# A two-block transformer layer kernel: the last stage's fixed experts in plain float32, and its weight ring eleven tiles deep

## The chip, the cores and the metric

The kernel runs on one core of a Trainium2 chip. The metric is the device time of one execution in microseconds, given as the median of several executions. The profile shows another, single execution; its span runs from the first to the last instruction of the program.

## The reference

Two blocks follow each other on 256 tokens of 1024 features, all in float32. The first has two layers with a recurrent and gated-linear-attention mixer each, a dense feed-forward in the one layer and 8 experts of which 2 are chosen in the other. The second block has a differential-attention and retention mixer, and then the part that matters here, 64 experts of width 256, of which each token uses 8:

```python
scores = sigmoid(h @ router_w)
sel = scores + router_bias
top_e = top 8 of sel within the 4 best of 8 groups
wts = scores[top_e] / sum * 2.5
for each expert e, over its tokens xb:
    yb = (silu(xb @ w1[e]) * (xb @ w3[e])) @ w2[e]
    acc[tok] += yb * wt
out = rmsnorm(x + g2 * (acc + shared(h)))
```

Every expert's weights are 3 MB (w1 and w3 in two tiles of 1 MB, w2 in one), so this stage loads 192 tiles of 1024 KB, 201 MB of the 647 MB that the whole kernel moves.

## The kernel before

**Weights** come through a ring (class `Ring`, lines 246 to 331): `add` lists the tiles in the order of their use, `load` (L260 to L270) takes a buffer and issues one 1 MB transfer on SyncE's queue (L269). The ring has seven buffers (tag `ring`). SyncE runs on its own: it issues the next transfer when the buffer that it needs has been read for the last time, and when its queue has come to it.

**Split or plain.** A tile marked `split` is cut into two halves ("granules"). For each, ScalarE writes the upper part (L366) and VectorE the rest (L367) into a buffer with tag `wsp`, of which there are four (8 KB a partition each, as large as a ring buffer). A product is then three matmuls on float32r parts (`mm3`, L373 to L378). A tile not marked so is used as it is, in plain float32 matmuls.

**Blocks of experts.** The routing gives each expert a place by its load (`by_load`), the first `NSTAT` experts excepted, which keep fixed places in front. `blocks2` (L2115) makes blocks of 128 rows: each of the 3 fixed experts has a block of its own (capacity 128), then 9 experts with 96 rows, 25 with 64 and 27 with 32 are packed two, three or four to a block. That makes 29 blocks. Which expert stands at a place is known only after the routing: VectorE writes it to `order`, and SyncE reads it from there before it issues the first tile of that expert (`moe2_tiles`, L2144). Tiles of fixed experts need no `order`: 8 tiles of the stage come ahead of the first that does.

**The order in a block.** `experts` (L1158) runs the blocks. TensorE computes the first product (`eh`) in two halves, a tile of each expert per half, and then the second product (`ey`) of the block before. Between the quarter steps it puts other jobs (`slots`): the gather of the tokens of later blocks (`gps`, L1138, and the transpose `PTp`, L1106), the transpose of the activation (`gT`, L1187) and the scatter of finished blocks (`sc`, L1249). Blocks with one expert are "heavy" (split weights, products `eh<-wsp` and `ey<-wsp`); the others are "light" (plain, `eh<-ringw` L1281 and `ey<-ringw` L1207) and run two or four column strips of the array side by side.

**Around the routing.** `moe2` (L1983) computes the router, then the shared expert (3 split tiles), between whose parts the gather of the first two blocks stands. It then loads tiles ahead (`ahead(RING)`, L2086), reads the overflow flag (L2087) and branches (L2088): only if an expert has more tokens than its place holds, a loop over all 64 experts runs (`dense_fallback`, L1337). Behind the branch come the 29 blocks. The four `wsp` buffers join the ring there (`wide`), for tiles that are asked for when no split tile is left in the list.

Of the kernel before, what the change touches and what calls it, by code (L numbers as in the profile page):

```python
# [21 lines left out]
NU = 11  # L22
NSTAT = 3
NBIG2 = 9
NMID2 = 25
LEAD1 = 4
RING = 7
NSPLIT = 4
# [217 lines left out]
class Ring:  # L246
# [3 lines left out]
    def __init__(self, k):  # L250
        self.k, self.order, self.at = k, [], 0
        self.ready, self.raw, self.gran, self.half, self.hold = [], [], [], None, False
        self.busy = 0
        self.wide = False
        self.n = 0

# [3 lines left out]
    def load(self):  # L260
        src, split = self.order[self.at]
        self.at += 1
        if callable(src):
            src = src()
        wide = self.wide and self.half is None and not any(sp for _, sp in self.ready + self.order[self.at - 1:])
        tag, bufs = ("ring", RING) if not wide or self.n % (RING + NSPLIT) < RING else ("wsp", NSPLIT)
        self.n += wide
        w = self.k.sb.tile([128, 2048], F32, name="ringw", tag=tag, bufs=bufs)
        self.k.nc.sync.dma_start(w, src)  # L269
        self.ready.append((w, split))  # L270

    def ahead(self, n):
# [61 lines left out]
class K:  # L334
# [739 lines left out]
    def gather_jobs(self, mp, ps, blks, moe, npt=3):  # L1074


        V, S, T = self.V, self.S, self.T
        xnh, xnl, A, B = [moe[k] for k in ("xnh", "xnl", "A", "B")]
        nb, deep = len(blks), 2
        n = 128 * nb  # L1080
        light = [len(blk["cols"]) > 1 for blk in blks]
        R = {}
# [75 lines left out]
    def experts(self, steps, moe, mp, ps, queue, extra, tail, slots, ys=None):  # L1158
# [9 lines left out]
        pend = None  # L1168
# [9 lines left out]
        def second(st):  # L1178

            G, u, y, n = st["G"], st["u"], st["y"], st["n"]  # L1180
            np_ = len(st["b"]["cols"])
            tiles = self.col_tiles(st["b"])

            def flip():
                b = ps.tile([128, 2, 128], F32, name="gT", tag="t", bufs=2)
                for f in range(2):
                    T.transpose(b[:, f], G[:, 128 * f:128 * f + 128], self.ident)  # L1187
                if np_ > 1:
                    st["g"] = mp.tile([128, 2, 128], F32, name="ghf", tag="gh", bufs=2)
                    S.copy(st["g"], b)  # L1190
                else:
                    gh = mp.tile([128, 2, 128], F32R, name="gh", tag="gh", bufs=2)
                    gl = mp.tile([128, 2, 128], F32R, name="glo", tag="glo", bufs=2)
                    S.copy(gh, b)
                    V.tensor_tensor(out=gl, in0=b, in1=gh.bitcast(F32), op=OP.subtract)
                    st["g"] = (gh, gl)

            def go(mid=None):
                if np_ > 1:
                    w2 = [self.ring.get() for _ in range(np_)]  # L1200
# [53 lines left out]
        for s, blk in enumerate(steps):  # L1254
# [10 lines left out]
            x, cols = blk["x"], blk["cols"]  # L1265
            n = len(cols)
            light = n > 1
            hb = ps.tile([128, 512], F32, name="eh", tag="h", bufs=2)
            go = None
            if pend is not None:  # L1270
                flip, go = second(pend)
                urgent.insert(0, flip)
                heavy0 = len(pend["b"]["cols"]) == 1
            for half in range(2):
# [35 lines left out]
            pend = this  # L1310
# [335 lines left out]
    def blocks1(self):  # L1646

        return [dict(cols=((k, 128),)) for k in range(4)], [dict(cols=((k, 64), (k + 1, 64))) for k in (4, 6)]

# [333 lines left out]
    def moe2(self, st, ss):  # L1983
        nc, tc, V, S, T, I, sb = self.nc, self.tc, self.V, self.S, self.T, self.I, self.sb
        A, B = st["A2"], st["B2"]
        with self.pool("me") as mp, self.pool("mep", PSUM) as ps, self.pool("eg") as gp:
# [8 lines left out]
            with self.pool("sh") as sp, self.pool("rt") as rp:  # L1995
# [69 lines left out]
                b = ps.tile([128, 512], F32, name="gtp", tag="t", bufs=2)  # L2065
# [19 lines left out]
                self.ring.hold = False  # L2085
                self.ring.ahead(RING)  # L2086
            fl = nc.values_load(flag[0:1, 0:1], min_val=0, max_val=64)  # L2087
# [4 lines left out]
            with self.pool("ex") as ep:  # L2092
# [8 lines left out]
                queue = [(i, lambda i=i: self.gather_jobs(gp, ps, steps[i + 2:i + 4], moe)) for i in range(0, len(steps) - 2, 2)]  # L2101
                self.ring.wide = True
                self.experts(steps, moe, ep, ps, queue, None, tail, SLOTS2)
# [11 lines left out]
    def blocks2(self):  # L2115

        big, mid = [list(range(a, a + n)) for a, n in ((NSTAT, NBIG2), (NSTAT + NBIG2, NMID2))]
        low = list(range(NSTAT + NBIG2 + NMID2, N2))
        kinds = [[], [], [], []]
        for k in big:  # L2120
            kinds[0].append(((k, 96), (low.pop(), 32)))
        if len(mid) % 2:
            kinds[1].append(((mid.pop(0), 64), (low.pop(), 32), (low.pop(), 32)))
        while mid:
            kinds[2].append(((mid.pop(0), 64), (mid.pop(0), 64)))
        assert len(low) % 4 == 0
        while low:
            kinds[3].append(tuple((low.pop(0), 32) for _ in range(4)))
        seq = sorted(((i + (0.5, 0.5, 0.5, 0.1)[n]) / len(kind), c) for n, kind in enumerate(kinds) for i, c in enumerate(kind))
        return [dict(cols=c) for c in [((k, 128),) for k in range(NSTAT)] + [c for _, c in seq]]  # L2130

# [12 lines left out]
    def moe2_tiles(self, fixed):  # L2144
# [20 lines left out]
        for k, i in (seq[:cut] if fixed else seq[cut:]):  # L2165
            self.ring.add([tile_of(k, i)], split=k < NSTAT)

# [120 lines left out]
```

## Time and profile before

| what | value |
|---|---|
| median of 3 executions | 2045.52 us (2044.01 to 2047.15) |
| profiled execution, its own time | 2043.03 us |
| its span | 2041.3 us, mean granted clock 0.976 |
| busy share of the span | TensorE 93%, VectorE 55%, ScalarE 42% |
| stage of the 64 experts, first issue of a tile to the end | 1464.9 to 2041.3 us |

The times in the rows below count from the span's start. A matmul's duration in the rows includes its overlap with the next one, so the distance between the starts of two neighbours is what one costs. A float32 matmul appears as two records. An issue on SyncE is not the transfer: the transfer lands later. "idle before" names what the engine waited for last.

### The profile page before, as it was taken

The numbers are of one execution on the slowest core, as the hardware profiler recorded it, in microseconds if no ns is written. First come the engines' busy times: TensorE is split into PE (matmuls) and PEld (weight loads), VectorE is DVE, ScalarE is ACT, GpSimd is POOL, SyncE is SP. The second block draws the span as 40 slices with busy tenths as digits, with TensorE's granted clock in tenths as the row PEclk, the third lists the DMA queues.
The fourth block names the chain that finished last, engine by engine and source line by source line (L and its number), as shares of the span: only waits on it lengthen the run. The fifth ranks groups of instructions, "written<-read, shape, count | busy, mean of one in ns | idle before, by whom it ended". The sixth has DMA issues, their size and how long they took to land. (4 is left out here: it accounts for less than half of the span.)

```text
span 2041.3 us, 26923 instructions
## 1 busy us (share of the span) xinstructions
PE 1891.7 (93%) x10218; PEld 1169.4 (57%) x10218; DVE 1115.6 (55%) x1787; ACT 860.0 (42%) x1383; POOL 107.0 (5%) x80
## 2 busy tenths in 40 slices
PE   6999999999799999999999997999877999999998
PEld 3777878675565555656556544887655433433333
DVE  4566544565565565556565524545676554545444
ACT  3646554464474454554454523533444222211112
POOL 0002330101100000000000001000100000000000
PEclk8999999999699999999999998999988999999999
DMA  9765665666479999989999997433524999999996
GB/s 395 271 227 214 241 264 205 245 245 228 183 294 402 419 365 404 418 357 405 420 418 420 420 419 305 165 124 125 191 94 186 407 419 419 420 419 419 419 420 263
DMA packets 90348, 646.76 MB, mean 317 GB/s; under 512 B 10100, under 2 KB 10388, under 8 KB 12392
## 3 DMA queue, kind: packets, MB, share of 16 engines
q1 hardware_dynamic: 88128, 638.62, 78.2%
q0 software_dynamic: 1312, 4.46, 0.6%
q8 instruction: 82, 1.34, 0.3%
q10 hardware_dynamic: 776, 1.93, 0.2%
q14 instruction: 50, 0.41, 0.1%
HBM read 643.92 MB, written 1.05 MB: 316 GB/s over the span
## 5 line engine op out<-in xcount | busy, mean ns | idle before, releaser
L367 DVE TENSOR_TENSOR wsp<-ringw,wsp 128x1024 fp32r<-128x1024 f32 x431 | 518.9, 1228 | 321.7 <-ACT wsp L366 318.7
L366 ACT CAST wsp<-ringw 128x1024 fp32r<-128x1024 f32 x442 | 452.4, 1046 | 216.1 <-DMA ringw<-in_wm_dram 110.6
L1281 PE MATMUL eh<-ringw,xe 128*64 128x512 f32 (+1 forms) x1984 | 385.1, 602 | 17.1 <-DMA ringw<-in_we_dram 17.1
L1281 PEld LDWEIGHTS eh<-ringw,xe 128*64 128x64 f32 (+1 forms) x1984 | 96.6, 124 | 219.8 <-issue 182.4
L1207 PE MATMUL ey<-ringw,ghf 128*64 128x512 f32 (+1 forms) x992 | 184.7, 600 | 7.1 <-DMA ringw<-in_we_dram 5.6
L376 PE MATMUL eh<-wsp,xe 128*128 128x512 f32 x360 | 150.0, 417 | 1.8 <-DVEq L1599 1.4
L1150 ACT ACTIVATE xe<-gps,mod,A 128x256 f32<-128x256 f32 (+1 forms) x60 | 32.5, 542 | 269.9 <-DVE xe L1148 269.9
L377 PE MATMUL eh<-wsp,xe 128*128 128x512 f32 x360 | 143.1, 398 | 3.2 <-DVE wsp L367 3.2
L1250 DVE TENSOR_TENSOR x<-x,sc 128x512 f32<-128x512 f32 x132 | 85.5, 684 | 105.8 <-PE sc L1249 105.8
L378 PE MATMUL eh<-wsp,xe 128*128 128x512 f32 x360 | 143.0, 397 | 0.0
L1207 PEld LDWEIGHTS ey<-ringw,ghf 128*64 128x64 f32 (+1 forms) x992 | 50.3, 125 | 108.9 <-issue 92.0
L689 PE MATMUL ps_h<-wsp,acth 128*128 128x256 f32 x544 | 103.8, 291 | 1.3 <-DVE kdec L1861 0.8
L1138 PE MATMUL gps<-P,xnh 128*128 128x256 f32 (+1 forms) x336 | 87.7, 297 | 9.6 <-DVE P L1097 5.2
L689 PEld LDWEIGHTS ps_h<-wsp,acth 128*128 128x128 f32 x544 | 85.7, 194 | 14.2 <-issue 11.6
L1138 PEld LDWEIGHTS gps<-P,xnh 128*128 128x128 f32 x336 | 66.1, 197 | 39.5 <-issue 33.6
L376 PEld LDWEIGHTS eh<-wsp,xe 128*128 128x128 f32 x360 | 68.8, 191 | 31.0 <-ACT wsp L366 9.4
L1148 DVE TENSOR_SCALAR xe<-gps,A,mod 128x256 f32<-128x256 f32 (+1 forms) x68 | 34.3, 504 | 91.7 <-PE gps L1138 87.7
L1138 PE MATMUL gps<-P,xnl 128*128 128x256 f32 (+1 forms) x336 | 83.9, 285 | 0.0
L477 PE MATMUL ada<-ringw,cT 128*32 128x512 f32 x512 | 67.3, 629 | 14.4 <-DMA ringw<-in_wada_dram 7.4
L1230 ACT CAST yh<-yg 128x512 fp32r<-128x512 f32 x70 | 42.9, 619 | 85.3 <-DVE yg L1229 85.2
L377 PEld LDWEIGHTS eh<-wsp,xe 128*128 128x128 f32 x360 | 69.0, 192 | 17.1 <-DVE wsp L367 5.0
L689 PE MATMUL ps_h<-wsp,actl 128*128 128x256 f32 x272 | 77.7, 286 | 0.2 <-DVE actl L637 0.2
(472 smaller groups left out, 3159.8 us busy)
## 6 DMA issues: line engine op xcount, KB each, us to landing
ringw<-in_wm_dram SPq DMA_DIRECT2D x264, 1024.0 KB, 10.4
ringw<-in_we_dram SPq DMA_DIRECT2D x192, 1024.0 KB, 18.9
ringw<-in_wd_dram SPq DMA_DIRECT2D x80, 1024.0 KB, 6.0
ringw<-in_wada_dram SPq DMA_DIRECT2D x72, 1024.0 KB, 5.5
x<-in_x_dram ACTq DMA_DIRECT2D x1, 1024.0 KB
wab<-in_wab_dram POOLq DMA_DIRECT2D x2, 512.0 KB, 9.1
xc<-in_xc_dram POOLq DMA_DIRECT2D x1, 1024.0 KB, 5.4
fg<-in_fg_dram POOLq DMA_DIRECT2D x2, 512.0 KB, 4.0
```

The costliest lines, as they stand in the source:

```text
L366: self.S.copy(hi, w)
L367: (eng or self.V).tensor_tensor(out=lo, in0=w, in1=hi.bitcast(F32), op=OP.subtract)
L376: mm(out, x[0], w[0], start=start, stop=False, skip_group_check=True)
L377: mm(out, x[0], w[1], start=False, stop=False, skip_group_check=True)
L378: mm(out, x[1], w[0], start=False, stop=stop, skip_group_check=True)
L477: T.matmul(st["acc"][32 * j:32 * j + 32, :], self.cT[l // 2][:, 4 // n * i + j // n, :], w[:, 512 * j:512 * j + 512], start=i == 0, stop=l ...
L689: mm(ps[:, t, :], x[a], b[:, o:o + 256], start=(d == 0 and t == 0 and i == 0), stop=(d == 7 and i == 2), skip_group_check=True)
L1138: T.matmul(b[:, d - d0], xx[:, t, 128 * d:128 * d + 128], R["P"][:, t, :n], start=i == 0, stop=i == 3, skip_group_check=True)
L1207: mm(y[cc][o:o + w, :], g[:, f, o:o + w], w2[e][:, 1024 * f + 512 * cc:1024 * f + 512 * cc + 512], start=u == 0 and f == 0, stop=u == n - ...
L1230: S.copy(yh[:, c], yg[cc])
L1250: V.tensor_tensor(out=self.x[:, t, c], in0=self.x[:, t, c], in1=b, op=OP.add)
L1281: mm(hb[o:o + w, :], x[:, d, o:o + w], ws[e][:, 512 * k:512 * k + 512], start=d == 0, stop=d == 7, skip_group_check=True)
```

## The change

Three things are changed, all in the last stage:

1. `NSTAT` is 2 instead of 3 and `NMID2` 24 instead of 25. The third fixed expert takes a place by its load like the others. There are 28 blocks: 2 with one expert, and as before 26 with two to four, 5 of them with four (before: 4 with four and 1 with three).
2. Every block of the stage has `whole=True`: the two one-expert blocks use plain float32 tiles over the whole array, without any split. The one-expert blocks of the first block's experts (`blocks1`) keep their split.
3. The ring is widened to 11 tiles (7 `ring`, 4 `wsp` buffers) by a call ahead of the branch, and 11 tiles are loaded there instead of 7. Only 5 tiles come ahead of the first that needs `order`.

```diff
-NSTAT = 3
+NSTAT = 2
 NBIG2 = 9
-NMID2 = 25
+NMID2 = 24
...
-        wide = self.wide and self.half is None and not any(sp for _, sp in self.ready + self.order[self.at - 1:])
-        tag, bufs = ("ring", RING) if not wide or self.n % (RING + NSPLIT) < RING else ("wsp", NSPLIT)
-        self.n += wide
+        tag, bufs = "ring", RING
+        if self.wide is not None:
+            if self.wide >= RING:
+                tag, bufs = "wsp", NSPLIT
+            self.wide = (self.wide + 1) % (RING + NSPLIT)
...
+    def widen(self):
+
+        assert self.half is None and not any(split for _, split in self.ready + self.order[self.at:])
+        self.wide = len(self.ready) + len(self.raw)
...
-        light = [len(blk["cols"]) > 1 for blk in blks]
+        light = [blk["whole"] for blk in blks]
...
-                if np_ > 1:
+                if whole:
...
-            light = n > 1
+            light = blk["whole"]
...
                 self.ring.hold = False
-                self.ring.ahead(RING)
+                self.ring.widen()
+                self.ring.ahead(RING + NSPLIT)
             fl = nc.values_load(flag[0:1, 0:1], min_val=0, max_val=64)
...
-                self.ring.wide = True
...
-        return [dict(cols=c) for c in [((k, 128),) for k in range(NSTAT)] + [c for _, c in seq]]
+        return [dict(cols=c, whole=True) for c in [((k, 128),) for k in range(NSTAT)] + [c for _, c in seq]]
...
-            self.ring.add([tile_of(k, i)], split=k < NSTAT)
+            self.ring.add([tile_of(k, i)], split=False)
```

SyncE's queue just ahead of the branch, in the kernel before (`ringw` is a tile of the ring, `in_we_dram` the experts' weights; a DMA waits for the engines that last used its buffer): the last four fixed tiles, then the flag.

```order
L269 DMA ringw<-in_we_dram 128x2048 [waits DMAHW7_49,DVE_49,Pool_49]
L269 DMA ringw<-in_we_dram 128x2048 [waits DMAHW0_49,Pool_49]
L269 DMA ringw<-in_we_dram 128x2048 [waits DMAHW1_49,DVE_49]
L269 DMA ringw<-in_we_dram 128x2048 [waits DMAHW2_49,DVE_49]
L2087 TENSOR_LOAD flag [waits DVE_49]
L2087 ISA x2
L2088 COMPARE_AND_BRANCH
```

The same queue in the changed kernel: five fixed tiles and two tiles that need `order` are ahead of these rows, and the four here go into the `wsp` buffers.

```order
L270 DMA ringw<-in_we_dram 128x2048 [waits PE_49]
L2157 TENSOR_LOAD order
L2157 ISA x2
L270 ISA
L270 DMA ringw<-in_we_dram 128x2048 [waits DMAHW2_49,PE_49]
L270 ISA
L270 DMA ringw<-in_we_dram 128x2048 [waits DMAHW3_49,PE_49]
L270 ISA
L270 DMA ringw<-in_we_dram 128x2048 [waits DMAHW4_49,PE_49]
L2096 TENSOR_LOAD flag [waits DVE_49]
L2096 ISA x2
L2097 COMPARE_AND_BRANCH
```

So the tiles that were asked for behind the branch, one by one as split buffers came free, are asked for ahead of it, and wait for TensorE's last reads of the shared expert instead of for VectorE's splits.

TensorE in the kernel before, in the second block: the last of its 24 split products of `eh`, then the first of the 12 of `ey` for the block before it.

```order
L376 MATMUL eh<-wsp,acth 128x512
L377 MATMUL eh<-wsp,acth 128x512
L378 MATMUL eh<-wsp,actl 128x512
L376 MATMUL ey<-wsp,gh 128x512
L377 MATMUL ey<-wsp,gh 128x512
L378 MATMUL ey<-wsp,glo 128x512
```

TensorE in the changed kernel: the end of the first block, the whole second block, and the first quarter of the third, which has four experts (32-row strips).

```order
L1113 MATMUL PTp<-cst,Pg 128x128 x4
L1288 MATMUL eh<-ringw,xe 128x512 x4
L1194 MATMUL gT<-cst,G 128x128 x2
L1288 MATMUL eh<-ringw,xe 128x512 x6
L1214 MATMUL ey<-ringw,ghf 128x512 x4
L1288 MATMUL eh<-ringw,xe 32x512 x8
```

A one-expert block has 8 products of `eh` and 4 of `ey`, where it had 24 and 12.

## Rows read from the trace of the kernel before

**Rows 1.** The page, part 2: GB/s moved in each of the 40 slices.

```profile
GB/s 395 271 227 214 241 264 205 245 245 228 183 294 402 419 365 404 418 357 405 420 418 420 420 419 305 165 124 125 191 94 186 407 419 419 420 419 419 419 420 263
```

**Rows 2.** Busy time by stretch of the last stage: engines, clock, DMA share, GB/s.

```profile
core 0: us, PE busy (x) PEld busy (x) DVE busy (x) ACT busy (x) POOL busy (x), PEclk, DMA share, GB/s
1464.00:1499.00 35.00, 29.54 (x158) 19.01 (x150) 23.27 (x70) 17.40 (x29) 7.82 (x4) 0.95 0.45 180
1499.00:1520.00 21.00, 12.42 (x68) 10.04 (x67) 17.84 (x36) 12.59 (x25) 0.58 (x1) 0.83 0.27 82
1520.00:1568.00 48.00, 37.26 (x164) 28.48 (x168) 36.68 (x83) 24.37 (x43) 0.00 (x0) 0.90 0.46 173
1568.00:1593.00 25.00, 22.34 (x125) 9.34 (x118) 13.60 (x27) 7.47 (x15) 0.00 (x0) 0.93 0.72 286
1593.00:2017.00 424.00, 403.76 (x2460) 160.45 (x2458) 208.99 (x483) 82.38 (x190) 0.00 (x0) 1.00 1.01 419
2017.00:2041.00 24.00, 14.99 (x79) 5.72 (x76) 10.75 (x17) 7.46 (x16) 3.24 (x3) 0.88 0.23 93
```

**Rows 3.** SyncE's issues of tiles to 1520 us; ns, first and last start.

```profile
L269 SPq DMA_DIRECT2D ringw<-in_we_dram x8: 327/328/328, 1464.9 to 1518.3; - x8
...
DMA to landing us min/median/max: 4.8/5.8/9.7
```

**Rows 4.** SyncE's issues of tiles from 1593 us; columns as before.

```profile
L269 SPq DMA_DIRECT2D ringw<-in_we_dram x164: 332/333/1148, 1592.8 to 2005.2; - x164
```

**Rows 5.** Waits from 1513 to 1568 us: total us, times, longest us.

```profile
DVE wsp L367 <- ACT wsp L366: 6.6, 6, 2.2
...
PE eh L376 <- ACTq L2088: 6.3, 1, 6.3
```

**Rows 6.** VectorE's groups, 1513 to 1568 us: busy us, mean ns, idle before.

```profile
L367 DVE TENSOR_TENSOR wsp<-ringw,wsp 128x1024 fp32r<-128x1024 f32 x16 | 19.5, 1222 | 7.4 <-ACT wsp L366 6.6 <-DMA ringw<-in_we_dram 0.6
```

**Rows 7.** VectorE's timeline around the branch: start us, us, instruction.

```profile
1513.89 1.22 DVE L367 TENSOR_TENSOR wsp<-ringw,wsp 128x1024 fp32r<-128x1024 f32 x1
...
1517.02 1.22 DVE L367 TENSOR_TENSOR wsp<-ringw,wsp 128x1024 fp32r<-128x1024 f32 x1
...
1518.16 0.68 DVE L1109 TENSOR_SCALAR PT<-PTp 128x512 fp32r<-128x512 f32 x1
```

**Rows 8.** VectorE's timeline where the experts' order is written.

```profile
1498.26 0.21 DVE L1472 CAST order<-ordp 1x64 int32<-1x64 f32 x1
```

**Rows 9.** TensorE's timeline around the branch, with idle time in brackets.

```profile
1513.12 0.60 PE L1106 MATMUL PTp<-cst,Pg 128*128 128x128 f32 x4
1519.99 0.80 PE L376 MATMUL eh<-wsp,acth 128*128 128x512 f32 x1 [6.27 <-ACTq L2088]
```

**Rows 10.** TensorE's timeline in split blocks: single products.

```profile
1544.71 0.63 PE L376 MATMUL eh<-wsp,acth 128*128 128x512 f32 x1
1545.13 0.63 PE L377 MATMUL eh<-wsp,acth 128*128 128x512 f32 x1
...
1548.54 0.39 PE L376 MATMUL eh<-wsp,acth 128*128 128x512 f32 x1
1548.76 0.39 PE L377 MATMUL eh<-wsp,acth 128*128 128x512 f32 x1
```

**Rows 11.** TensorE's timeline: four plain float32 products over the whole array.

```profile
1493.58 3.59 PE L529 MATMUL ada<-adrow,cst 128*128 128x512 f32 x8
```

**Rows 12.** The chain of waits, 1495 to 1600 us: start us, us, what.

```profile
1563.23 1.88 PE gps L1138 x16
```

**Rows 13.** TensorE's timeline in blocks of plain float32 experts.

```profile
1567.85 1.92 PE L1281 MATMUL eh<-ringw,xe 128*32 128x512 f32 x16
...
1624.13 1.89 PE L1281 MATMUL eh<-ringw,xe 128*64 128x512 f32 x8
...
1639.68 1.90 PE L1281 MATMUL eh<-ringw,xe 128*32 128x512 f32 x16
```

**Rows 14.** TensorE's timeline at the stage's end.

```profile
2022.11 5.51 PE L1207 MATMUL ey<-ringw,ghf 128*32 128x512 f32 x32
```

More of the change, by code (lines that the diff above doesn't have):

```diff
@@ L253, in __init__ @@
         self.busy = 0
-        self.wide = False
-        self.n = 0
+        self.wide = None
     def add(self, srcs, split=True):
@@ L1180, in second @@
             G, u, y, n = st["G"], st["u"], st["y"], st["n"]
-            np_ = len(st["b"]["cols"])
+            np_, whole = len(st["b"]["cols"]), st["b"]["whole"]
             tiles = self.col_tiles(st["b"])
@@ L1198, in go @@
             def go(mid=None):
-                if np_ > 1:
+                if whole:
                     w2 = [self.ring.get() for _ in range(np_)]
@@ L1272, in experts @@
                 urgent.insert(0, flip)
-                heavy0 = len(pend["b"]["cols"]) == 1
+                heavy0 = not pend["b"]["whole"]
             for half in range(2):
@@ L1646, in blocks1 @@
     def blocks1(self):
-        return [dict(cols=((k, 128),)) for k in range(4)], [dict(cols=((k, 64), (k + 1, 64))) for k in (4, 6)]
+        return ([dict(cols=((k, 128),), whole=False) for k in range(4)],
+                [dict(cols=((k, 64), (k + 1, 64)), whole=True) for k in (4, 6)])
     def steps1(self):
@@ L2118, in blocks2 @@
         low = list(range(NSTAT + NBIG2 + NMID2, N2))
[L2119 to L2123, printed above, removed]
+        kinds = [[((k, 96), (low.pop(), 32)) for k in big], [], []]
         while mid:
-            kinds[2].append(((mid.pop(0), 64), (mid.pop(0), 64)))
-        assert len(low) % 4 == 0
+            kinds[1].append(((mid.pop(0), 64), (mid.pop(0), 64)))
         while low:
-            kinds[3].append(tuple((low.pop(0), 32) for _ in range(4)))
-        seq = sorted(((i + (0.5, 0.5, 0.5, 0.1)[n]) / len(kind), c) for n, kind in enumerate(kinds) for i, c in enumerate(kind))
-        return [dict(cols=c) for c in [((k, 128),) for k in range(NSTAT)] + [c for _, c in seq]]
+            kinds[2].append(tuple((low.pop(0), 32) for _ in range(4)))
+        seq = sorted(((i + (0.5, 0.5, 0.1)[n]) / len(kind), c) for n, kind in enumerate(kinds) for i, c in enumerate(kind))
+        return [dict(cols=c, whole=True) for c in [((k, 128),) for k in range(NSTAT)] + [c for _, c in seq]]
     def units(self, src, n, between=None):
```

## The prediction

> **What bounds the kernel now.** I read the slices first. In the last nine or so, from the stage of the 64 experts on, the rate stands at 419 to 420 GB/s, and the slice before them falls to 186 [rows 1]. So the question is when the stream of the stage becomes full and what keeps it from that. The stretches of the stage answer the first half: from 1593 to 2017 us the DMA share is 1.01 at 419 GB/s, while it is 0.27, 0.46 and 0.72 in the three stretches from 1499 to 1593 [rows 2]. A tile of 1024 KB is 1.049 MB, so at 419 GB/s one lands every 2.50 us. SyncE's issues confirm that tiles are then asked for as fast as they can come: 164 of the 192 are issued from 1592.8 to 2005.2 us, one per 2.5 us [rows 4].
>
> How far is the stream at 1593? Behind that, 424 us at 419 GB/s are 177.7 MB or 169.4 tiles; the last stretch moves 2.2 MB, of which 1.05 MB is the output, so another 1.1 tiles [rows 2]. Of 192, then, 170.5 are still to come and 21.5 have landed. Whatever makes this count larger at 1593 takes 2.50 us per tile off the end, as long as the stream stays full and TensorE keeps up behind it.
>
> What holds the stream back before 1593 is the second half. Only 8 tiles are issued to 1520 us, with up to 4.8 us (alone) to 9.7 us to land [rows 3]: that is all that seven buffers and the splits allow. Then the three split blocks run at the pace of VectorE and ScalarE: 16 splits of 1.22 us on VectorE between 1513 and 1568, which wait 6.6 us for ScalarE's half [rows 5, 6], and a ring buffer comes free only when its tile has been split. Three such blocks take from 1519.99 to 1567.85 us, 48 us [rows 9, 13]. TensorE itself is idle for 6.3 us at the branch [rows 5, 9].
>
> **The change, part by part.**
>
> *Removed splits.* No tile of the stage is split any more; what is left of these instructions belongs to the shared expert. The two splits of 1.22 us that stand ahead of the branch on VectorE (1513.89, 1517.02) delay `PT` at 1518.16 [rows 7], ScalarE's sums follow it, and TensorE's first product waits for them until 1519.99 [rows 9]. Without both, TensorE starts 2.4 us earlier, at 1517.5. It can't start ahead of 1513.7, where its own work ends, and it need not be later than now: bounds 1513.7 and 1520.
>
> *Plain products.* A split product costs 0.23 us (1548.54 to 1548.76), and twice that at the lower clock (1544.71 to 1545.13, 0.42) [rows 10]. A one-expert block has 36: 8.2 us. Four plain float32 products over the whole array take 3.59 us as a group with the tail of the last, 0.85 us each [rows 11]; a block has 12: 10.2 us. The Trainium skill, page "FP8 and Floating Point Precision", section "TensorE Precision Notes", says that true float32 makes four passes through the array. This speaks against the change, and the two rows agree with it (0.85 against 0.23): if TensorE's products set the time, two blocks would cost 4 us more than two split ones. But they don't set it here: three split blocks are 25 us of products in a stretch of 48 us, and it is the rest that goes.
>
> *First block.* 8 products of `eh` at 0.85 are 6.8 us; the gather of the next two blocks is 32 `gps` at 0.118 (16 in 1.88 us [rows 12]), 3.8 us; the transposes 0.5 us. TensorE comes from a pause, and the granted clock was 0.90 in the stretch from 1520 [rows 2], so I add 2 us for products at 1.2 GHz. Sum 13 us: 1517.5 to 1530.5. *Second block:* 6.8 us, the transpose 0.4 us and 4 products of `ey`, 3.4 us: to 1541.1. *Third block* (four experts): its first half is two quarters of 1.9 us [rows 13] and a transpose of 0.4 us, to 1545.4.
>
> *The ring.* VectorE writes `order` at 1498.5 [rows 8], as before. From there SyncE asks for tiles 6 to 11; the last two need the buffers that TensorE reads last for the shared expert, ahead of the row at 1513.12 [rows 9], so they go at about 1514 and land by 1520. Nothing is issued on the queue in front of them that is late. The first of the three moved tiles loses something: tile 6 was issued at 1484.2 and now waits for `order` until 1499, but is needed only at 1541; cost nothing. From then on tile k+11 is asked for when tile k has been read: 12 to 16 one by one through the first two blocks, and 17 to 20 together at 1545.4, when the first half of the third block is done. This is where the stream becomes full: 17 lands at 1545.4 + 4.8 = 1550.2, and 20 at 1557.7. The next four buffers come free with the second half, two quarters and two scatters later at about 1551, ahead of 1552.9, at which they must be asked for to leave no hole.
>
> *The sum.* At 1593 the changed kernel has 17 + (1593 - 1550.2) / 2.50 = 34.1 tiles, against 21.5: 12.6 more, 31.5 us. At the end, before, TensorE lags behind the stream: its last `ey` ends at 2027.6 [rows 14]. Four blocks of two experts now follow the last block of four, where five did, and each takes TensorE 15.55 us (1624.13 to 1639.68 [rows 13]) against 6 x 2.50 = 15.0 us for the stream, so the lag shrinks by 0.5 us. The tail from 2027.6 to 2041.3 stays. Gain 32 us. Does TensorE keep up? 26 blocks of 15.55 us are 404 us, from 1541 to 1945; the stream ends at 1550.2 + 175 x 2.50 = 1988. It does. Span 2041.3 - 32 = 2009; the profiled execution's own time was 2043.0, which gives 2011. The median of the runs stands 2.5 us above that execution, so I say **2013.5 us**.
>
> *Bounds.* What no row shows is how long the two plain blocks take from the branch on. With all their 24 products at the lower clock (0.85 us more each) the third block starts 20 us later and the gain is 12 us: 2034. If the stream were full from the eleventh tile on, at 1520, it would have 11 + 73 / 2.50 = 40 tiles at 1593, and the gain would be 47 us: 1999.
>
> **The rivals.**
>
> *A. The ramp has holes.* Buffers come free in bursts; before, too, the stretch from 1568 to 1593 was at a share of 0.72 only [rows 2], which is 7 us lost in 25. If the change keeps such a stretch, or the two blocks stay at 1.2 GHz for a good part, the gain is 20 to 25 us: about 2023. For it: the gaps of TensorE just there, the granted clock of 0.83 from 1499 to 1520. Against: two blocks without a wait for a split. The Trainium skill, page "TensorE: Matmul & The Clock Gate", section "What's actually happening", has the throttled clock as the default that activity releases; the rows at 1544 and 1548 agree [rows 10].
>
> *B. The stream is full earlier*, since the first half of block one frees buffers sooner than I think: 1999 to 2006. Against: four tiles can't be asked for together before the third block, which has four experts.
>
> *C. Slower: the branch is taken.* A place's capacity is now 96 from the third on and 32 from the 36th on (38th before). If one expert has more tokens than its place holds, the loop over 64 experts runs, with 192 loads into one buffer of at least 4.8 us each [rows 3]: 920 us more, near 2930. It decides from 97 tokens at the third place, 65 at the 12th or 33 at the 36th. The reference's routing of its own inputs gives 87, 50 and 27 there, so this needs other inputs.
>
> *D. The change does not do what it says*: the stage's end hangs on something besides the stream, or SyncE is held by the extra reads of `order`. Then 2040 to 2046. Against: a share of 1.01 for 424 us, and both queues as printed above.
>
> **How the numbers follow.** Forecast 2013.5, with 2007 to 2019 as its own range: 0.66. A 0.20, B 0.08, C 0.02, D 0.04. For 8 in 10 I take the forecast's range, most of A and a part of B: 2005 to 2025. A measurement of this kernel tells about 0.2% (4 us) from no change: faster by more than that has the forecast, A and B and a part of D, 0.95; within it D's rest, 0.03; slower C, 0.02.
>
> **What would show it.** Right: eleven issues of tiles by 1516 us; TensorE's first product at about 1517.5; the first products with 32-row strips at about 1541 (1567.85 before [rows 13]); a DMA share near 1 from 1550 on; the last `ey` near 1996. Wrong in size: a third block that starts later than 1550, or stretches with a share below 0.9 behind it. Wrong in kind: a full stream from 1550 but an end later than 2020, which would mean that TensorE or the tail has become the bound.

## The result and the profile after

The changed kernel takes **2012.88 us** (median of 4, 2010.10 to 2017.09), the kernel before beside it 2046.34 us (4 runs, 2044.01 to 2050.97): a ratio of 0.9835, 95% interval 0.9811 to 0.9860, so 33 us faster. The profiled execution took 2012.2 us, with a span of 2010.4 us.

The slices of the page, as in [rows 1]: eight of the last nine stand at 419 to 420 GB/s (the last, 269, holds the end), and the low stretch ahead of them is now five slices between 110 and 182, then 291.

```profile
GB/s 395 282 226 214 251 251 205 268 201 219 221 239 401 419 384 384 420 403 352 421 419 419 420 419 388 182 160 126 110 157 291 420 419 419 419 419 419 419 419 269
```

The stretches of the last stage, to be laid beside [rows 2] (the last stretch of full stream is cut at 1700 here):

```profile
core 0: us, PE busy (x) PEld busy (x) DVE busy (x) ACT busy (x) POOL busy (x), PEclk, DMA share, GB/s
1464.00:1499.00 35.00, 30.03 (x154) 19.13 (x152) 22.40 (x69) 16.35 (x28) 7.83 (x4) 0.95 0.38 151
1499.00:1520.00 21.00, 15.17 (x81) 11.95 (x79) 18.05 (x45) 7.48 (x14) 0.58 (x1) 0.87 0.74 269
1520.00:1568.00 48.00, 47.35 (x221) 22.44 (x222) 21.50 (x55) 9.50 (x21) 0.00 (x0) 0.98 0.78 306
1568.00:1593.00 25.00, 25.00 (x178) 10.60 (x174) 14.44 (x35) 6.41 (x15) 0.00 (x0) 1.00 1.01 420
1593.00:1700.00 107.00, 104.35 (x640) 42.05 (x640) 55.69 (x137) 21.36 (x49) 0.00 (x0) 1.00 1.01 419
1700.00:2010.00 310.00, 283.29 (x1684) 109.85 (x1682) 146.86 (x327) 61.55 (x141) 3.23 (x3) 0.99 0.96 395
```

From 1520 to 1568 us TensorE is busy for 47.35 of 48 us (37.26 before), and the DMA share is 0.78 (0.46). From 1568 on the stream is full; before, that stretch was at 0.72. SyncE's issues of tiles to 1516 us, as in [rows 3]:

```profile
L270 SPq DMA_DIRECT2D ringw<-in_we_dram x11: 327/333/346, 1466.7 to 1515.1; - x11
...
DMA to landing us min/median/max: 4.7/7.7/9.7
```

Eleven, where eight had gone by 1520. TensorE's timeline from the branch to the first block of four experts, for [rows 9, 13]:

```profile
1514.93 0.60 PE L1113 MATMUL PTp<-cst,Pg 128*128 128x128 f32 x4
1518.65 3.38 PE L1288 MATMUL eh<-ringw,xe 128*128 128x512 f32 x4 [3.12 <-ACTq L2097]
...
1530.35 3.60 PE L1288 MATMUL eh<-ringw,xe 128*128 128x512 f32 x8
1533.79 0.38 PE L1194 MATMUL gT<-cst,G 128*128 128x128 f32 x2
1534.00 5.32 PE L1288 MATMUL eh<-ringw,xe 128*128 128x512 f32 x12
1539.16 3.60 PE L1214 MATMUL ey<-ringw,ghf 128*128 128x512 f32 x8
1542.68 1.92 PE L1288 MATMUL eh<-ringw,xe 128*32 128x512 f32 x16
```

A plain product is two records, so the group at 1530.35 has four products: the last two of block one's `eh` and the first two of block two's, which starts in its middle, at 1532.1. The `gT` at 1533.79 is block one's activation, the `ey` at 1539.16 is block one's second product, and the first product with 32-row strips starts at 1542.68 (1567.85 before [rows 13]). VectorE's `PT` ([rows 7] before, with a split on either side of it) and the last product of the experts ([rows 14] before):

```profile
1516.47 0.68 DVE L1116 TENSOR_SCALAR PT<-PTp 128x512 fp32r<-128x512 f32 x1
```

```profile
1990.20 6.27 PE L1214 MATMUL ey<-ringw,ghf 128*32 128x512 f32 x32
```

### The profile page after: what moved, and what is told of

Read it like the earlier page. It is cut to its first block, busy times and chain, and to the rows that moved or that the text cites. A ratio compares the mean times of both kernels' runs of the same rounds, so it can differ in the third digit from the quotient of the medians.

```text
span 2010.4 us, 26598 instructions
## 1 busy us (share of the span) xinstructions
PE 1879.5 (93%) x10114; PEld 1154.8 (57%) x10114; DVE 1083.0 (54%) x1736; ACT 830.7 (41%) x1331; POOL 107.0 (5%) x80
## 5 line engine op out<-in xcount | busy, mean ns | idle before, releaser
L373 DVE TENSOR_TENSOR wsp<-ringw,wsp 128x1024 fp32r<-128x1024 f32 x413 | 497.0, 1228 | 308.7 <-ACT wsp L372 302.8
L372 ACT CAST wsp<-ringw 128x1024 fp32r<-128x1024 f32 x424 | 434.0, 1046 | 205.8 <-DMA ringw<-in_wm_dram 110.4
L1288 PE MATMUL eh<-ringw,xe 128*64 128x512 f32 (+2 forms) x2016 | 398.1, 601 | 19.5 <-DMA ringw<-in_we_dram 15.6
L1288 PEld LDWEIGHTS eh<-ringw,xe 128*64 128x64 f32 (+2 forms) x2016 | 102.8, 125 | 227.9 <-issue 188.3
L1214 PE MATMUL ey<-ringw,ghf 128*64 128x512 f32 (+2 forms) x1008 | 190.8, 600 | 5.7 <-DMA ringw<-in_we_dram 4.6
L382 PE MATMUL eh<-wsp,xe 128*128 128x512 f32 x352 | 146.6, 416 | 1.8 <-DVEq L1606 1.4
L383 PE MATMUL eh<-wsp,xe 128*128 128x512 f32 x352 | 140.1, 398 | 3.2 <-DVE wsp L373 3.2
L384 PE MATMUL eh<-wsp,xe 128*128 128x512 f32 x352 | 139.9, 398 | 0.0
L1214 PEld LDWEIGHTS ey<-ringw,ghf 128*64 128x64 f32 (+2 forms) x1008 | 53.7, 126 | 110.8 <-issue 96.4
L1145 PEld LDWEIGHTS gps<-P,xnh 128*128 128x128 f32 x320 | 63.6, 199 | 35.6 <-issue 30.6
L1155 DVE TENSOR_SCALAR xe<-gps,A,mod 128x256 f32<-128x256 f32 (+1 forms) x64 | 33.7, 527 | 88.9 <-PE gps L1145 88.9
L382 PE MATMUL fh<-wsp,acth 128*128 128x512 f32 x192 | 77.6, 404 | 0.0
## 6 DMA issues: line engine op xcount, KB each, us to landing
ringw<-in_wm_dram SPq DMA_DIRECT2D x264, 1024.0 KB, 10.1
```

The source lines that it names most:

```text
L372: self.S.copy(hi, w)
L373: (eng or self.V).tensor_tensor(out=lo, in0=w, in1=hi.bitcast(F32), op=OP.subtract)
L382: mm(out, x[0], w[0], start=start, stop=False, skip_group_check=True)
L383: mm(out, x[0], w[1], start=False, stop=False, skip_group_check=True)
L384: mm(out, x[1], w[0], start=False, stop=stop, skip_group_check=True)
L1145: T.matmul(b[:, d - d0], xx[:, t, 128 * d:128 * d + 128], R["P"][:, t, :n], start=i == 0, stop=i == 3, skip_group_check=True)
```

## The experiments

The theory: in the full stream a tile lands every 2.50 us, so the time is set by how many tiles have landed when the stream is full for good. The rivals give the gain to TensorE (a block less, less work), to one part of the change alone, or to the ring's depth alone. Since each kernel's stream should be full from 1593 or so on, one row of a view tests the theory in all of them: the rate from 1450 to 1700 us, a stretch of 250 us. One GB/s more there is 0.25 MB, at 419 GB/s 0.60 us. The row of each kernel, with the row behind it where the stream differs; first before, after, and the changed kernel once more:

```profile
1450.00:1700.00 250.00, 216.34 (x1201) 117.41 (x1199) 154.58 (x354) 87.27 (x171) 8.39 (x5) 0.95 0.71 283
1700.00:1960.00 260.00, 246.21 (x1486) 97.41 (x1483) 127.98 (x306) 49.97 (x115) 0.00 (x0) 1.00 1.01 419
```

```profile
1450.00:1700.00 250.00, 234.76 (x1321) 116.39 (x1320) 141.85 (x352) 66.83 (x137) 9.61 (x7) 0.98 0.83 333
1700.00:1960.00 260.00, 242.46 (x1450) 95.04 (x1449) 124.02 (x291) 48.69 (x112) 0.00 (x0) 1.00 1.01 419
```

```profile
1450.00:1700.00 250.00, 236.32 (x1325) 119.86 (x1325) 143.04 (x352) 68.44 (x139) 10.59 (x7) 0.97 0.81 325
```

Two fixed experts, split (e1); no splits only (e2); joined behind the branch (e3); seven deep (e4, two rows):

```profile
1450.00:1700.00 250.00, 220.91 (x1233) 116.83 (x1232) 146.18 (x342) 79.31 (x154) 9.13 (x7) 0.94 0.75 300
```

```profile
1450.00:1700.00 250.00, 234.16 (x1248) 118.87 (x1246) 138.18 (x335) 65.13 (x134) 8.79 (x6) 0.95 0.77 309
```

```profile
1450.00:1700.00 250.00, 236.53 (x1328) 120.74 (x1328) 142.77 (x352) 68.18 (x138) 10.58 (x7) 0.97 0.80 324
```

```profile
1450.00:1700.00 250.00, 228.29 (x1241) 113.10 (x1239) 135.38 (x332) 64.08 (x131) 10.59 (x7) 0.97 0.77 309
1700.00:1960.00 260.00, 243.16 (x1454) 96.15 (x1452) 124.25 (x295) 49.19 (x113) 0.00 (x0) 0.99 0.99 408
```

Three fixed, eleven deep (e5); extra buffers joined late (e10); one, none, and none once more (e7, e6, e12); two fixed side by side (e9); half of `ey` left out (e8, two rows):

```profile
1450.00:1700.00 250.00, 235.05 (x1291) 121.81 (x1292) 141.29 (x340) 68.33 (x138) 10.59 (x7) 0.97 0.78 311
```

```profile
1450.00:1700.00 250.00, 228.85 (x1251) 114.62 (x1251) 135.85 (x332) 65.30 (x132) 10.58 (x7) 0.97 0.76 308
```

```profile
1450.00:1700.00 250.00, 232.16 (x1346) 113.56 (x1345) 140.17 (x351) 65.30 (x135) 8.88 (x6) 0.97 0.83 337
```

```profile
1450.00:1700.00 250.00, 224.80 (x1315) 106.75 (x1318) 132.67 (x336) 63.09 (x130) 9.39 (x7) 0.97 0.83 341
```

```profile
1450.00:1700.00 250.00, 225.13 (x1316) 107.20 (x1318) 132.73 (x336) 63.32 (x130) 9.55 (x7) 0.97 0.83 341
```

```profile
1450.00:1700.00 250.00, 229.73 (x1290) 109.95 (x1289) 133.50 (x335) 61.56 (x129) 8.37 (x5) 0.95 0.83 337
```

```profile
1450.00:1700.00 250.00, 229.38 (x1239) 110.78 (x1242) 139.25 (x353) 65.20 (x140) 8.39 (x5) 0.98 0.84 342
1700.00:1960.00 260.00, 231.84 (x1294) 89.89 (x1290) 122.08 (x291) 48.15 (x112) 0.00 (x0) 0.99 1.01 419
```

All of it in one table. "Worth" is the rate less 283, times 250 / 419. The stage runs from the first issue of one of its tiles to the end of the last `ey`, in the profiled execution; where the first tile waits for the routing it can't be compared. The last column runs from VectorE's write of `order` to the same end.

| kernel | median, us | ratio to before (95%) | rate, GB/s | worth, us | span | span gained | stage, us | from `order`, us |
|---|---|---|---|---|---|---|---|
| before | 2044.6 to 2046.3 | 1 | 283 | 0 | 2041.3 | 0 | 562.7 | 529.4 |
| changed kernel | 2012.88 | 0.9835 (0.9811 to 0.9860) | 333 | 29.8 | 2010.4 | 30.9 | 529.7 | 496.4 |
| e11, the same again | 2014.56 | 0.9844 (0.9827 to 0.9861) | 325 | 25.1 | 2015.1 | 26.2 | 530.5 | 497.5 |
| e1 | 2031.85 | 0.9938 (0.9925 to 0.9951) | 300 | 10.1 | 2030.0 | 11.3 | 549.7 | 516.8 |
| e2 | 2027.72 | 0.9900 (0.9887 to 0.9914) | 309 | 15.5 | 2026.1 | 15.2 | 546.5 | 510.7 |
| e3 | 2015.46 | 0.9847 (0.9835 to 0.9860) | 324 | 24.5 | 2015.6 | 25.7 | 530.2 | 497.2 |
| e4 | 2031.42 | 0.9929 (0.9916 to 0.9942) | 309 | 15.5 | 2030.2 | 11.1 | 547.5 | 514.4 |
| e5 | 2024.25 | 0.9895 (0.9880 to 0.9911) | 311 | 16.7 | 2024.7 | 16.6 | 539.4 | 506.4 |
| e10 | 2024.08 | 0.9892 (0.9873 to 0.9911) | 308 | 14.9 | 2025.6 | 15.7 | 540.7 | 507.7 |
| e7 | 2010.76 | 0.9835 (0.9822 to 0.9849) | 337 | 32.2 | 2008.3 | 33.0 | 528.1 | 494.7 |
| e6 | 2008.77 | 0.9826 (0.9811 to 0.9841) | 341 | 34.6 | 2005.7 | 35.6 | - | 492.6 |
| e12, e6 again | 2007.34 | 0.9822 (0.9804 to 0.9840) | 341 | 34.6 | 2005.6 | 35.7 | - | 492.3 |
| e9 | 2010.49 | 0.9831 (0.9816 to 0.9845) | 337 | 32.2 | 2008.7 | 32.6 | 529.7 | 493.9 |
| e8 | 2002.38 | 0.9790 (0.9776 to 0.9803) | 342 | 35.2 | 1999.8 | 41.5 | 527.6 | 494.3 |

In every kernel but e4 and e8 the worth of the tiles landed by 1700 us gives the span gained to within 1.3 us. The exceptions have their own rows, below. The row tells when a gain is made and not by what: any cause that acts ahead of 1700 us would agree with it, and the causes are told apart by the edits below. One caution: the first issue of the stage lies anywhere from 1464.9 us (before) to 1471.7 (e5) in executions whose instructions ahead of it are the same. Up to 6.8 us of a single span, and of a rate with it, is that; so parts of the change are compared by the stage. That does not remove everything. In e2 and e9 VectorE writes `order` 35.8 us behind the first issue, in the other kernels with fixed experts 32.9 to 33.4: from 1480 to 1485 us the granted clock was 0.50 there, and TensorE's work up to `order` took some 2.5 us longer. The first block's gather stands behind the routing, so the table has as well the time from the write of `order` to the end of the last `ey`; the changed kernel and e11, its equal, differ by 1.1 us in it. The write and that stretch, in the changed kernel and in e9:

```profile
1500.10 0.21 DVE L1479 CAST order<-ordp 1x64 int32<-1x64 f32 x1
1480.00:1485.00 5.00, 4.54 (x25) 3.74 (x24) 2.58 (x19) 2.09 (x4) 3.75 (x2) 0.95 0.15 62
```

```profile
1500.82 0.21 DVE L1479 CAST order<-ordp 1x64 int32<-1x64 f32 x1
1480.00:1485.00 5.00, 4.54 (x14) 3.25 (x13) 3.22 (x18) 1.57 (x3) 3.52 (x2) 0.50 0.00 0
```

### The parts of the change (e1, e2, e5, e10)

**e1**, the packing alone:

```diff
-NSTAT = 3
+NSTAT = 2
-NMID2 = 25
+NMID2 = 24
```

> The kernel before with only the packing of the change (two fixed experts instead of three, 28 blocks), split blocks and ring as before. Theory (the end is set by how many tiles of the last stage have landed when its stream becomes full, 2.50 us per tile): the plain blocks begin one split block earlier, 16 us, but with three tiles fewer consumed (7.5 us), so about 8.5 us come off the kernel before: 2037, ratio 0.996. Rival 1 (one block of TensorE's work less is what the change gains): 16 us or more, 2030, and with the plain products another 16. Rival 2 (the packing does not matter): 2046.

Measured 2031.85 us, 13.0 us off the stage. More than the theory's 8.5, less than rival 1's 16. The 32-strip products begin at 1551.25, 16.6 us earlier than before, as expected; the DMA share is 0.75 in the 25 us behind that point, hardly better than the 0.72 of before [rows 2]. Of the 4.5 us above the theory 1.4 are the end: the last `ey` is done 11.2 us behind the landing of tile 189, before it was 12.5. Where the rest comes from was not tried.

**e2**, the splits alone (the tests for a block's width ask for `whole`, as in the change):

```diff
...
-        return [dict(cols=c) for c in [((k, 128),) for k in range(NSTAT)] + [c for _, c in seq]]
+        return [dict(cols=c, whole=True) for c in [((k, 128),) for k in range(NSTAT)] + [c for _, c in seq]]
...
-            self.ring.add([tile_of(k, i)], split=k < NSTAT)
+            self.ring.add([tile_of(k, i)], split=False)
```

> The kernel before with only the splits of the last stage removed: three fixed experts as before, plain, and the ring widened behind the branch as before. Theory: the wait for splits was the cost, so most of the gain comes with this alone: the first 32-strip product at about 1553.5, the tile nine behind it landing at 1562.6, 32.2 tiles at 1593 against 21.5 before, 27 us off: 2019, ratio 0.987. Rival 1 (the gain comes with the early eleven-deep loading): under 10 us off, 2038. Rival 2 (plain products cost more than the split ones that they replace): no gain or slower.

Measured 2027.72: 16.2 us off the stage (18.7 from `order`), not 27. Rival 2 is out, since plain products pay; but nearly half of the gain is missing. In the rule of the kernel before, seven more tiles go into the seven buffers before the four extra ones are used, and this expectation had left that out.

**e5** adds to e2 the rule of the change, by which the extra buffers take the very next tiles:

```diff
-                self.ring.ahead(RING)
+                self.ring.widen()
+                self.ring.ahead(RING + NSPLIT)
...
-                self.ring.wide = True
```

> The changed kernel with three fixed experts again (29 blocks, one of them of three experts), plain and eleven deep. It is the kernel with only the splits removed plus the change's rule by which the four extra buffers take the very next tiles; in that kernel, as before, they join only after seven more. Theory (tiles landed by 1700 us set the end): the blocks of several experts begin one plain block later than in the changed kernel, 11 us, with three tiles more consumed, 7.5 us, so 3.5 us worse than the changed kernel: about 2016, and 11 us better than the kernel with the splits alone removed. Rival 1 (that kernel is slow because of its three blocks, the rule means nothing): 2027. Rival 2 (the number of fixed experts means nothing): 2013.

Measured 2024.25, only 3.5 us below e2, and the intervals of the two ratios overlap; it is 7.1 us off e2's stage, but 4.3 from `order`. So this run alone does not put rival 1 out; that the rule counts rests on e10, below. The third fixed expert counts, so rival 2 is out. The stage is 9.7 us longer than the changed kernel's instead of 3.5, in part because the third plain block took longer than the 11 us allowed:

```profile
1548.23 1.88 PE L1288 MATMUL eh<-ringw,xe 128*128 128x512 f32 x4
...
1555.47 1.88 PE L1288 MATMUL eh<-ringw,xe 128*128 128x512 f32 x4
...
1559.06 3.60 PE L1214 MATMUL ey<-ringw,ghf 128*128 128x512 f32 x8
1562.59 1.92 PE L1288 MATMUL eh<-ringw,xe 128*32 128x512 f32 x16
```

From 1548.23 to 1562.59 are 14.4 us. Besides its own products this block has the second product of the block before and, between the quarters, the scatters of a finished one and a part of a gather. That is 3.4 of the 6.2 us that the expectation is off by; 1.4 more are the end (the last `ey` 12.5 us behind the landing of tile 189, 11.1 in the changed kernel), and the rest is open.

**e10**, the changed kernel with the old rule:

```diff
     def widen(self):
-        self.wide = len(self.ready) + len(self.raw)
+        self.wide = 0
...
-                self.ring.widen()
-                self.ring.ahead(RING + NSPLIT)
+                self.ring.ahead(RING)
...
+                self.ring.widen()
                 self.experts(steps, moe, ep, ps, queue, None, tail, SLOTS2)
```

> The changed kernel with the joining rule of the kernel before: seven tiles ahead of the branch, the next seven into the same seven buffers, and only then four into the extra ones. Theory: until the fifteenth tile this is the ring of seven, so its ramp is that of the run with seven throughout (70 to 71 tiles at 1700, relative to the start of the stage), but from there on the stream has no holes: 10 us worse than the changed kernel, 8 better than seven throughout, 2023. Rival (the whole cost of seven lies in later holes, not in the ramp): 2013.

As the theory says: 2024.08, stage 540.7, and beside it e11 has 2014.56. With e1 this gives one path through the change in stage time: packing 13.0 us (562.7 to 549.7), no splits 9.0 (to 540.7), extra buffers at once 11.0 (to 529.7); from `order` 12.6, 9.1 and 11.3. On the other path, by e2 and e5, it is 16.2 for the splits, 7.1 for the buffers and 9.7 for the packing; from `order`, without e2's late routing, 18.7, 4.3 and 10.0. So no part is the gain: each is worth between an eighth and a good half of it, depending on which came first.

### Where and how deep the ring is widened (e3, e4)

**e3** calls `widen` behind the branch and loads seven tiles ahead of it.

```diff
-                self.ring.widen()
-                self.ring.ahead(RING + NSPLIT)
+                self.ring.ahead(RING)
...
+                self.ring.widen()
                 self.experts(steps, moe, ep, ps, queue, None, tail, SLOTS2)
```

> The changed kernel with seven tiles loaded ahead of the branch and the four other buffers joined behind it. Theory: these four tiles are asked for some 3 to 10 us later, but land by 1530 and are not needed before 1540, and tiles from the twelfth on hang on TensorE's reads alone: 2013 to 2014, the same as the changed kernel. Rival (loading eleven early is part of the gain): four tiles or 10 us worse, 2023.

Its stage is 530.2 us, that of the changed kernel 529.7 and 530.5. The place ahead of the branch is worth nothing here; that the four buffers take the next tiles is.

**e4** leaves the call out and stays at seven buffers.

```diff
-                self.ring.widen()
-                self.ring.ahead(RING + NSPLIT)
+                self.ring.ahead(RING)
```

> The changed kernel with a ring of seven to the end of the stage (four buffers of the splits unused). Theory: at the first block of four experts 12 tiles have been asked for instead of 16, which is 10 us, and the blocks of four leave holes in a stream that only seven buffers feed: 10 to 20 us worse than the changed kernel, about 2028. Rival (depth does not matter once the splits are gone): 2013.

2031.42, 18 us worse. The ramp is e10's (rate 309 and 308), and the rest is the later rate: 408 GB/s from 1700 to 1960 where every other kernel has 419, which over some 300 us is about 8 us of stream. Against e10 it costs 6.8 us of stage.

### Fewer fixed experts (e7, e6, e12) and two in one block (e9)

**e7** and **e6** go on in the direction of the change, with `NSTAT = 1`, `NMID2 = 23` (and the kernel before's block of three experts) and `NSTAT = 0`, `NMID2 = 22`.

> The changed kernel with one fixed expert, 27 blocks, one of them of three experts. Theory: two tiles land ahead of the routing, tiles 12 and 13 come late because the one plain block gives back its two buffers 6 us apart, and the stream is full from tile 14, at 1541: 77.6 tiles at 1700 against 75.9, 4 us better than the changed kernel: 2009. Rival 1 (fixed tiles ahead of the routing are worth their 2.5 us each): 6 us worse, 2019. Rival 2 (a block less of TensorE's work counts): 12 us better, 2001.

> The changed kernel with no fixed expert at all: 26 blocks of two to four, places by load from the first on, no tile of the stage ahead of the routing. Theory: eleven tiles are asked for from 1501 us on, one lands every 2.50 us from 1506 on, and since the first block has four experts TensorE gives buffers back four at a time from about 1523, so the stream never pauses again: 78.6 tiles at 1700 against 75.9, 7 us better than the changed kernel: 2006. Rival 1 (the early fixed tiles and plain blocks cover the routing's latency, without them TensorE stands): 5 tiles less, 12 us worse, 2025. Rival 2 (two blocks less of TensorE's work is what counts): 2 x 12 us better, 1989.

2010.76 (494.7 us from `order`) and 2008.77: both rivals are out in both cases. With no fixed expert no tile of the stage lands before 1500 us, and it is no loss. The stretches of e6 show a stream that is full from the branch on:

```profile
1520.00:1545.00 25.00, 23.37 (x140) 8.78 (x140) 5.76 (x17) 4.35 (x11) 0.00 (x0) 0.93 1.01 417
1545.00:1568.00 23.00, 21.18 (x141) 7.86 (x142) 12.80 (x38) 4.17 (x8) 0.00 (x0) 1.00 1.01 419
```

The size is smaller than expected: from VectorE's write of `order` to the end of the last `ey` it is 492.6 us, in the changed kernel 496.4 (e11: 497.5), so 4 to 5 us and not 7. The fourth tile landed at 1515.2 us; the expectation had 1513.5.

> The kernel with no fixed expert once more, since its first median (2008.77) lies only 4 to 6 us below the two of the changed kernel (2012.88, 2014.56). Theory (its stream is full from the fourth tile on, 1.5 to 2 tiles ahead of the changed kernel): 3 to 5 us better than the changed kernel again, 2009, ratio 0.982 to 0.983. Rival (the difference was scatter of what runs ahead of the stage): 2013 to 2014, ratio 0.984 to 0.985.

2007.34, and 492.3 us from `order` on. The intervals of the ratios still overlap with those of the changed kernel, but two medians of e6 (2008.8, 2007.3) lie below three of the changed kernel and of e3, its equal (2012.9, 2014.6, 2015.5), and the traces agree with the size. I take it as 4 us better.

**e9** puts the two fixed experts side by side in one block.

```diff
-    cap[:NSTAT] = 128.0
+    cap[:NSTAT] = 64.0
...
-... [((k, 128),) for k in range(NSTAT)] ...
+... [tuple((k, 64) for k in range(j, j + 2)) for j in range(0, NSTAT, 2)] ...
```

> The changed kernel with its two fixed experts side by side in one block (64 rows each, so a capacity of 64 instead of 128), 27 blocks. Theory (what counts is how many tiles have landed when the stream is full for good): four tiles land ahead of the routing instead of five, but the first block gives its buffers back two at a time and the block of four experts comes 13 us earlier, so the stream is full from tile 14, landing at about 1533: 80.8 tiles at 1700 against 75.9, 12 us better than the changed kernel: 2001. Rival 1 (the first block stands at the lower clock and the stream has holes to the first block of four): 77 tiles as with no fixed expert, 2009. Rival 2 (the ramp is already as good as it gets, the end hangs on something else): 2013.

2010.49, and rival 1 had 2009. The stage, 529.7 us, is that of the changed kernel, but it has the late routing in it: from `order` on it is 493.9 us against 496.4 and 497.5, so 2 to 4 us are gained and not 12. The medians say the same (e11 beside it: 2014.56), with intervals that overlap. The estimate had left out what stands between the products of the first block. TensorE's timeline, without most of the gather:

```profile
1516.78 0.66 PE L1113 MATMUL PTp<-cst,Pg 128*128 128x128 f32 x4
1521.32 3.68 PE L1288 MATMUL eh<-ringw,xe 128*64 128x512 f32 x8 [3.89 <-ACTq L2097]
...
1526.87 1.94 PE L1288 MATMUL eh<-ringw,xe 128*64 128x512 f32 x8
...
1530.80 1.94 PE L1288 MATMUL eh<-ringw,xe 128*64 128x512 f32 x8
...
1534.24 3.79 PE L1288 MATMUL eh<-ringw,xe 128*64 128x512 f32 x24
...
1538.34 5.36 PE L1288 MATMUL eh<-ringw,xe 128*32 128x512 f32 x48
```

```profile
1520.00:1525.00 5.00, 3.68 (x9) 0.84 (x9) 1.36 (x8) 0.86 (x4) 0.00 (x0) 0.50 0.83 331
1525.00:1530.00 5.00, 5.00 (x27) 3.47 (x27) 0.56 (x2) 0.56 (x1) 0.00 (x0) 0.83 0.10 18
1530.00:1535.00 5.00, 5.00 (x32) 2.90 (x32) 3.85 (x12) 1.64 (x3) 0.00 (x0) 1.00 0.93 380
```

It starts 20.5 us behind `order` (18.6 in the changed kernel), its first four products (eight records) run at a granted clock of 0.50 and take 3.68 us, where the next four take 1.94, and 24 `gps` lie ahead of 1530.80. The first half's buffers are asked for again only at 1528.8, and for 5 us the stream stands (share 0.10). The block of four begins in the group at 1534.24, behind the first block's last eight records, at about 1536: 6 us later than I had put it. That is rival 1's mechanism, and it costs most of what the packing could have gained.

### TensorE's work (e8)

```diff
                         for cc in range(2):
+                            if f == 1 and np_ > 1:
+                                continue
                             for e, o, w in tiles:
...
-                                   stop=u == n - 1 and f == 1, skip_group_check=True)
+                                   stop=u == n - 1 and (f == 1 or np_ > 1), skip_group_check=True)
```

> The changed kernel, in which the second half of the second product is left out in the 26 blocks of several experts (those matmuls are not computed): some 49 us less work for TensorE (26 x 1.9 us), every tile loaded as before. Theory (the stream sets the end, TensorE has slack behind it): 2010 to 2013, only the last blocks behind the last tile get shorter. Rival (TensorE, busy for 93% of the span, sets it, so the change gained by taking work from it): up to 49 us off, 1964.

The median is 2002.38, but the edit also reached the two-expert blocks of the first block's experts, and the stage begins at 1458.3 us, 8.4 us earlier than in the changed kernel. The stage itself is 527.6 us: 2.1 us shorter (2.1 from `order` too), with the busy time of `ey` in those blocks down from 101 to 56 us. The waits of TensorE from 1593 to 2000 us show where a part of that went; first the changed kernel, then e8:

```profile
PE eh L1288 <- DMA ringw<-in_we_dram: 15.6, 15, 2.6
PE ey L1214 <- DMA ringw<-in_we_dram: 4.6, 4, 1.5
```

```profile
PE eh L1290 <- DMA ringw<-in_we_dram: 32.7, 28, 2.1
PE ey L1216 <- DMA ringw<-in_we_dram: 7.2, 5, 2.2
```

20.2 us of waiting for tiles have become 39.9. TensorE, busy for 93% of the span, does not set the end of this stage; the rival falls. That e8's span gains 6.3 us more than its rate is worth has two reasons: 1.44 MB more had been moved ahead of 1450 us (3.4 us), and the last `ey` is done 9.5 us behind the landing of tile 189 instead of 12.5.

## Why the prediction was right

Times of the changed kernel are later by 1.9 us from the first issue of the stage on (1466.75 against 1464.9); they are compared with that taken off.

- *The stream as the bound, 2.50 us per tile.* Right: 419 GB/s from 1593 on, in the table to within 1.3 us, and e8.
- *TensorE's restart.* Predicted 1517.5, measured 1518.65, so 1516.8 on the old count. `PT` starts at 1516.47, 1.7 us earlier than before although the stage runs 1.9 us late, with no split beside it.
- *The two plain blocks.* Predicted 13 and 10.6 us, measured 13.4 (1518.65 to 1532.1) and 10.6 (to 1542.68). Of the 2 us for the lower clock 1.5 were there: the first two products take 3.38 us, later pairs 1.88. In e11, the same kernel, the two blocks take 25.5 us instead of 24.0, so a match this close is in part luck.
- *The ring.* Eleven issues by 1515.1, as predicted. Tiles 17 to 20 were asked for from 1546.8 to 1548.6 and the 17th landed at 1551.8 (predicted 1550.2 without the shift). One hole was missed, 1.3 us between tiles 18 and 19. The count at 1593 was 32.9, with the shift taken off 33.7; predicted 34.1.
- *The end.* The last `ey` ends at 1996.47, 1994.6 on the old count (predicted 1996). The lag behind the stream shrank more than the 0.5 us that I gave it: from the landing of tile 189 to the last `ey` it is 11.1 us, 12.5 before.
- *Sum.* Gain of the span 30.9 against 32 (33.0 by the stage, which leaves the late start out), and 2012.88 against 2013.5 for the median.
- *The rivals.* A's stretch is there but small (0.96 from 1545 to 1568: 0.77 to 1550, 1.01 behind it), B's did not come, C's branch was not taken, D is out.

What did not stand is the part ahead of the sum, "what holds the stream back before 1593 is the second half" with its splits. The sum was worked forward through the changed kernel and needs no shares, so it came out; but as an account of the kernel before it is half of the story. Without splits and with all else as before the stage gains 16.2 of 33.0 us, 18.7 counted from `order`. Nor do the splits hold back the tiles issued up to 1520 us, as it says of these eight: e2, with seven buffers and no split, has issued only seven by then and the eighth at 1527.2, since a split gives its ring buffer back ahead of TensorE's product (SyncE waits for VectorE's `wsp` before, for TensorE's `eh` in e2). The rest is the rule by which the extra buffers join, which the prediction used (tile k + 11) without saying that it differs from before, and the blocks with one expert, which hold the stream back without a split too.

## What to carry to other kernels

When a stage ends at the rate of its stream, count what has landed at the moment from which the stream stays full; the cost of everything ahead is read from that count, and the busy share of the compute engine says nothing of it. In a ramp, look at how fast each step gives buffers back, and order steps so that those that free the most per us come first; extra buffers have to take the very next loads, or they join too late. Parts of such a change overlap, so the worth of one part depends on what has been done already.

## What had not been expected of the hardware

- A plain float32 product over the whole array costs as much time as four side by side on 32-row strips: two of the former take 1.88 us (1534.00 group: six in 5.32), eight of the latter 1.92 us (1542.68). So a block with one expert gives back a tile per 3.5 to 4.8 us (three in 10.6 to 14.4), one with four gives back a tile per 1.3 us (12 in 15.5), and the stream brings one per 2.5. This fits e6, which gains by having no fixed expert although no tile lands early.
- Time from issue to landing grows with the tiles asked for: 4.7 us for a tile alone, 19.6 us (median, 1600 to 1960) with eleven buffers, 9.9 with seven. The rates differ by 419 to 408 GB/s only.
- Executions differ by up to 6.8 us in when the last stage begins, with the same instructions ahead of it (two executions of the changed kernel by 4.0). In one profile that is a fifth of this change's gain.
